# A one-layer encoder block on one core: latents turned in pieces, small first transfers, a tail in two tiles, weight halves side by side for the rotary key, and a second Strassen pair for B's output

## The chip, the core and the metric

The kernel runs on one core of a Trainium2 chip. The metric is the device time of one launch in microseconds (us). Three runs of the kernel before took 2494.61 to 2496.06 us, with a median of 2495.51. The core has five engines that run instruction streams of their own and in their own order: TensorE (PE, matmuls and transposes), VectorE (DVE), ScalarE (ACT), GpSimd (POOL) and SyncE (SP, here only a queue for transfers). An instruction that waits on its engine holds everything behind it on that engine.

## The reference

The block works on 256 tokens of width 2048 in float32. Cut to what matters:

```python
h = LN(alpha*h + 0.5*swiglu_ffn(h, ffn1_w_in, ffn1_w_out))      # d_ff 5504
proj = h @ w_in              # q, k, v of A | q_lat 512 | kv_lat 512 | k_pe 64 | gates
y_a = chunked_relbias_attention(q, k, v, rel_bias) @ w_o_a      # 16 heads of 64
c_q, c_kv = rms_norm(q_lat, q_a_norm), rms_norm(kv_lat, kv_a_norm)
k_pe = apply_rope(k_pe)                                         # one rotary key for all heads
y_b = mla_attention(c_q @ w_q_b, c_kv @ w_kv_b, k_pe) @ w_o_b   # 16 heads
h = LN(alpha*h + (sig(g_a)*y_a + sig(g_b)*y_b) @ w_out)
h = LN(alpha*h + cross_attention(h, LN(mem)))                   # 4 heads, 256 tokens of memory
out = LN(alpha*h + 0.5*swiglu_ffn(h, ffn2_w_in, ffn2_w_out))
```

## The kernel before

**Numbers in two halves.** Every operand of a matmul, weight or activation, is split into a high and a low half in the type fp32r, hi + lo. A product is three matmul passes: hi by hi, hi by lo, lo by hi. ACT casts the high half from the raw weights in casts of 1,024 columns (L242, in `halves`) and DVE subtracts to get the low half, 2,048 columns in one instruction (L245). For activations `split` does the same (L234, L235).

**Weights.** All weights stream once from memory, in 1 MB tiles of 128 rows by 2,048 columns (`raw`, three buffers) issued on SP's queue. `run` walks a list of items made with `add`; each item names the weights that it needs, and `run` fetches and splits weights ahead of it, with two units of hi and lo in flight. An item can have a priority: a positive one (SOON 400, NEAR 100) lets the scheduler put its instructions earlier among those of its engine, a negative one (LATE) later. The order on each engine is fixed when the kernel is built.

**Strassen pairs.** In a group of products (`pair_group`), the weights of two column blocks are multiplied with both token halves, eight products of blocks with three matmuls each, 24 matmuls of 512 columns for a step of two rows of weight blocks. At chosen steps (the tables `SUMS_...`) the group uses Strassen's seven products, 21 matmuls (`mm_sums`). Such a step needs sums of weight blocks (DVE, L189 and L191 in `form_sums`), a second split of these sums (ACT L242 and DVE L245 into a tile named X), and sums of the activations made once for all groups (`sum_forms`, called by `forms_step`). After the last such step `shared` joins the seven products (L627 to L632). `SUMS_YB` is the table of B's output projection, whose two groups are built by `out_b`; it has one pair, step 4.

**Wide products.** Where one weight tile turns features into features (`mm_wide`), the activation's hi and lo halves lie side by side, so that the high weights take 16 matmuls of 512 columns (L265) and the low weights 16 matmuls of 256 columns (L267), into the left half of the same bank. `total` adds the two halves of the bank (L273, L274).

**Start.** `start` runs 12 warm-up matmuls of ones (L475; the trace has two records for each), while the input `xT` (8 blocks of 256 KB) is asked for on ACT's queue (L483) and the first weights on SP's (L486, the first two tiles in halves). For each block it splits the input and then the weights, the high halves all on ACT, and multiplies.

**The mixer.** The order is: value and gates, then the latents (`w_lat`, whose product `lat_scale` scales by the root mean square, DVE L857 to L865), `gb_apply(0)`, the rotary key (`kpe`), A's first projections (`a_proj(0)`), `lat_turn`, A's heads and then B's heads. `lat_turn` turns the scaled latents with 16 transposes (L877), two into each bank half, and splits them from the bank: ACT for hi (L881) and DVE for lo (L882). B's projections read its result. `kpe` multiplies with `mm_wide`; its weight tile holds the 64 columns of the key twice, so that the 128 rows of the result are two copies. `swap` (L891) fetches a copy with neighbouring blocks of 32 rows exchanged, by four transfers on SP's queue; DVE multiplies by cosine and sine (L898, L899) and adds into `krope` (L902), which only B's scores (L924) read. `gb_apply(0)` applies the first norm's gain and bias to the residual `h`: for each quarter of 512 columns two broadcasts on POOL's queue (L440, L441) and four DVE operations (L444, L445).

**B's heads.** A loop over 16 heads issues for each the scores, the softmax on DVE and ACT (`softmax`), the transposes of the head before (L774), the projections of a head two ahead, and the head's output. After it come `out_a`, `out_b` and, beside B's output, the norm of the memory (`mem_norm`: statistics on DVE, L377 and L1167, spread over the partitions by PE at L1174).

**The end.** The last feed-forward's output is built by `out_pair` (columns 0 to 1,023) and `out_proj` (columns 1,024 to 2,047, groups of four weight blocks). `skewed` runs the last four weight groups for token half 0 first and then for token half 1, so that the first half's norm runs beside the second's matmuls. The last group of half 1 is 9 matmuls of 512 columns (L286); then DVE adds it to `h` (L701), takes the statistics (L377), joins them (L382), and `final_steps` normalizes and stores (L1320, L1321).

Of the kernel before, what the change touches and what calls it, by code (L numbers as in the profile page):

```python
# [91 lines left out]
class Kernel:  # L92
    def __init__(self, ctx, tc, t, out):
        self.tc, self.nc, self.t, self.out = tc, tc.nc, t, out

        def pool(name, bufs=1, **kw):
            return ctx.enter_context(tc.tile_pool(name=name, bufs=bufs, **kw))

        self.const = pool("const")
        self.wraw = pool("wraw", 3)  # L100
        self.whi = pool("whi", UNITS)
        self.wlo = pool("wlo", UNITS)
        self.blocks = pool("blocks")
# [7 lines left out]
        self.chain = None  # L111


# [165 lines left out]

    def mm_tok(self, ps, tt, w, x, kts, start, stop):  # L280

        n = len(kts)
        for wi in range(2):
            for j, kt in enumerate(kts):
                for xi in range(2 - wi):
                    self.last_mm = self.nc.tensor.matmul(  # L286
                        ps, x.at(xi, kt)[:, tt * P:(tt + 1) * P], w[wi][:, j * 512:(j + 1) * 512],
                        start=(start and j + wi + xi == 0), stop=(stop and j == n - 1 and wi == 1),
                    )
# [82 lines left out]

    def ln_begin(self):
        return self.small.tile([P, 4, 6], F32, tag="bn", name=self.name("bn"))

# [93 lines left out]
    def start(self):  # L469
# [6 lines left out]
        ps = self.group_tiles(0)  # L476
        xr = self.block("H0", (P, KT // 2, S)), self.block("H1", (P, KT // 2, S))
        for k in range(KT // 2):
            v = xr[k // 4][:, k % 4 * 2:k % 4 * 2 + 2, :]
# [12 lines left out]
            self.mm_pair(ps, w, 512, xT, (2 * k, 2 * k + 1), k == 0, k == KT // 2 - 1)  # L492
# [18 lines left out]
    def ffn(self, tag, xT, st, first=None, steps=None, late=None, before=None, tags=None):  # L511
# [6 lines left out]
        for half, nf in enumerate(F_SPLIT):  # L518
# [25 lines left out]
            if end and late:  # L544
                self.add(late)

            def out(hid=hid):
# [4 lines left out]
                if end:  # L552
                    self.out_proj(tag + "_w_out_r", nf, x, False, st, steps, tags, 2)
                else:
                    self.out_pair(bank ^ 1, src[1], 1, nf, x, homes, fh, half == 0, None)
# [139 lines left out]
    def finish(self, tt, n, ps, scale, st):  # L695
# [6 lines left out]
        if st is not None:  # L702
            if n == 0:
                st[tt] = self.ln_begin()
            self.ln_piece(st[tt], h[tt], n)

    def out_proj(self, wname, nk, x, scale, st, steps=None, tags=None, n0=0, other=False):

# [12 lines left out]
        def part(n, tts, i, ps, tags=None, held=0, keep=False, again=False):  # L721
            grp = groups[i]

            def fn(w=None):
                if keep:
                    kept[i] = w
                w = kept.pop(i) if again else w
                for tt in tts:
                    if i == 0:
                        ps[tt] = self.at_tile() if other and n == n0 else self.mm_tile()  # L730
                    self.mm_tok(ps[tt], tt, w, x(), grp, i == 0, i == len(groups) - 1)
                if i == len(groups) - 1:
# [51 lines left out]
    def mixer(self, xT, st, steps):  # L784
# [83 lines left out]

        def lat_turn():
            self.c = self.act(["X0", "X1"])  # L870
            for k in range(2):
                for b in range(2):
                    ps = self.at_tile()
                    for i in range(2):
                        j, p = 2 * b + i, ps[:, i * S:(i + 1) * S]
                        for tt in range(2):
                            nc.tensor.transpose(p[:, tt * P:(tt + 1) * P],  # L877
                                                self.lat[:, tt, k, j * P:(j + 1) * P], self.ident)
                        gain = self.vec(("q_a_norm", "kv_a_norm")[k], j)
                        hi, lo = (self.c.at(half, 4 * k + j) for half in (0, 1))  # L880
                        nc.scalar.mul(hi, p, gain)  # L881
                        nc.vector.scalar_tensor_tensor(lo, p, gain, hi.bitcast(F32), ALU.mult, ALU.subtract)  # L882

        self.pair_group(0, t["w_lat"][0], 512, KT, xT, SUMS_IN, fx, lps, lqs, None, SUM_HOME + ("H5",))
        self.add(lat_scale, prio=SOON)
        self.add(lambda: self.gb_apply(0, self.h), prio=LATE)

        def swap(dst, src):

            for b in range(4):  # L890
                nc.sync.dma_start(dst[32 * b:32 * b + 32], src[32 * (b ^ 1):32 * (b ^ 1) + 32])  # L891

        def kpe(w):
            ps = self.at_tile()
            self.mm_wide(ps, w, xT())
            a, b = self.total(ps), self.w1()
            swap(b, a)
            nc.vector.tensor_tensor(a, a, self.rope[:, 0, :], ALU.mult)  # L898
            nc.vector.tensor_tensor(b, b, self.rope[:, 1, :], ALU.mult)  # L899
            for j in range(2):  # L900
                rows = slice(64 * j, 64 * j + 64)
                nc.vector.tensor_tensor(self.krope[rows, j, :], a[rows], b[rows], ALU.add)  # L902
        self.add(kpe, t["w_kpe"][0])


        qk, sc, pt = {}, {}, {}
        oA = {}

        def a_proj(i):
            def one(k):  # L910
# [5 lines left out]
            for k in range(2):  # L916
                self.add(one(k), t["w_qk"][i, k])

        def scores(parts, spans_q):
# [82 lines left out]
        a_proj(0)  # L1002
        self.add(lat_turn)
        NA = A_HEADS // 2
# [69 lines left out]
        for h in range(B_HEADS + 1):  # L1074
# [8 lines left out]
            if h > 0:  # L1083
                b_out(h - 1, int(h % 2 == 0 and h + 2 < B_HEADS))


# [376 lines left out]
```

## Time and profile before

| What | Value |
|---|---|
| Runs, median and extent | 2495.51 us (2494.61 to 2496.06) |
| The profiled execution's own time | 2493.65 us |
| Its span | 2491.9 us |
| PE busy | 2471.8 us, 11,966 records |
| DVE busy | 2055.1 us, 82% |
| ACT busy | 1332.9 us, 53% |
| Memory read | 484.77 MB, 195 GB/s over the span |
| Clock granted to PE | full in all 40 slices |

In the timeline a row is the start in us, the length in us, engine, line, operation, output and inputs, the number of instructions in the row, and in brackets the idle time of the engine ahead of it with what released it. Successive matmuls overlap: the record of one with 512 columns is 0.39 us long, while the starts lie closer together. In the groups of instructions the numbers after the bar are the total busy us, the mean ns of one, and the idle time ahead. Windows list, for each stretch, the busy time of each engine with the number of records, then the clock, the share of the transfer engines and GB/s.

### The profile page before, as it was taken

To read this page: it belongs to the slowest core of one execution; us is meant where nothing else is said; L and a number is where in the kernel's file an instruction comes from. 1 tells how busy PE (TensorE), PEld (TensorE's weight loads), DVE (VectorE), ACT (ScalarE), POOL (GpSimd) and SP (SyncE) were. 2 spreads that over 40 slices of the span, in tenths; PEclk is the share of its full clock that TensorE was granted. 3 is DMA by queue.
4 is the path that set the end of the run, shared out by engine and by line. 5 is a ranking of instruction groups with operands and counts; after the bars stand their busy time and mean duration, and the time that the engine had idled before them with its cause. 6 is when DMAs were issued, how large, how long until landed. Compare 5 with 4: busy or idle time off the path is not lost.

```text
span 2491.9 us, 30464 instructions
## 1 busy us (share of the span) xinstructions
PE 2471.8 (99%) x11966; PEld 2082.8 (84%) x11966; DVE 2055.1 (82%) x2313; ACT 1332.9 (53%) x1798; POOL 28.8 (1%) x69
## 2 busy tenths in 40 slices
PE   9999999999999999999999999999999999999998
PEld 7888888889888888899888888898888888888886
DVE  6999889899778988676678798557888988898986
ACT  5555555555455555555445565545555555555552
POOL 0000000000000001000000000000000000000000
PEclk9999999999999999999999999999999999999999
DMA  7655555556645556543466557544555555655664
GB/s 255 240 191 208 188 201 209 203 186 204 236 160 203 210 203 226 199 153 119 168 221 219 186 175 247 189 167 148 205 204 186 203 186 203 210 198 201 206 211 141
DMA packets 72512, 490.03 MB, mean 197 GB/s; under 512 B 8368, under 2 KB 8752, under 8 KB 17200
## 3 DMA queue, kind: packets, MB, share of 16 engines
q1 hardware_dynamic: 66384, 467.11, 53.7%
q0 software_dynamic: 4256, 17.83, 2.2%
q10 hardware_dynamic: 1728, 3.15, 0.4%
q8 instruction: 93, 1.52, 0.2%
q14 instruction: 51, 0.42, 0.0%
HBM read 484.77 MB, written 2.10 MB: 195 GB/s over the span
## 4 chain that ended last, share of the span: by engine, by line
PE 95%; DVE 2%; DMA 1%; ACT 1%; issue 0%; SPq 0%; DVEq 0%; ACTq 0%; POOL 0%
PE mm L299 25%; PE at L299 25%; PE mm L353 10%; PE at L353 10%; PE mm L286 8%; PE mm L265 7%; PE mm L267 4%; PE mm L255 2%; PE at L924 1%; PE at L286 1%; DVE lo L245 1%; PE at L774 1%; DMA H<-xT 0%; PE at L1279 0%; PE at L404 0%; PE at L1255 0%
## 5 line engine op out<-in xcount | busy, mean ns | idle before, releaser
L242 ACT CAST hi<-raw 128x1024 fp32r<-128x1024 f32 (+1 forms) x848 | 801.8, 987 | 604.2 <-PE at L299 182.6
L245 DVE TENSOR_TENSOR lo<-raw,hi 128x2048 fp32r<-128x2048 f32 (+2 forms) x425 | 904.3, 2129 | 239.6 <-ACT hi L242 237.8
L299 PE MATMUL mm<-hi,T 128*128 128x512 f32 (+1 forms) x1280 | 298.4, 383 | 1.4 <-ACT hi L234 1.4
L242 ACT CAST X<-H 128x1024 fp32r<-128x1024 f32 (+1 forms) x162 | 164.9, 1034 | 216.7 <-DVE H L191 86.6
L299 PEld LDWEIGHTS mm<-hi,T 128*128 128x128 f32 x1280 | 238.0, 188 | 46.1 <-ACT hi L234 2.0
L299 PE MATMUL at<-hi,T 128*128 128x512 f32 x1072 | 257.0, 389 | 0.0
L245 DVE TENSOR_TENSOR X<-H,X 128x2048 fp32r<-128x2048 f32 (+1 forms) x81 | 182.3, 2251 | 67.7 <-ACT X L242 67.7
L299 PEld LDWEIGHTS at<-hi,T 128*128 128x128 f32 x1072 | 201.2, 188 | 41.9
L299 PE MATMUL mm<-lo,T 128*128 128x512 f32 (+1 forms) x640 | 153.8, 382 | 0.0
L299 PE MATMUL at<-hi,H 128*128 128x512 f32 x608 | 144.7, 390 | 0.9 <-DVE w L632 0.9
L299 PEld LDWEIGHTS mm<-lo,T 128*128 128x128 f32 x640 | 119.1, 188 | 21.8
L299 PEld LDWEIGHTS at<-hi,H 128*128 128x128 f32 x608 | 113.9, 188 | 24.7 <-DVE w L632 1.3
L299 PE MATMUL at<-lo,T 128*128 128x512 f32 x536 | 132.6, 389 | 0.0
L265 PE MATMUL mm<-T,hi 128*128 128x512 f32 x512 | 124.4, 394 | 0.0
L299 PEld LDWEIGHTS at<-lo,T 128*128 128x128 f32 x536 | 100.6, 188 | 20.9
L299 PE MATMUL mm<-hi,H 128*128 128x512 f32 x480 | 116.1, 392 | 0.0
L191 DVE TENSOR_TENSOR H<-H,raw 128x512 f32<-128x512 f32 (+1 forms) x162 | 109.5, 676 | 1.7
L265 PEld LDWEIGHTS mm<-T,hi 128*128 128x128 f32 x512 | 94.2, 189 | 19.3 <-issue 0.9
L299 PEld LDWEIGHTS mm<-hi,H 128*128 128x128 f32 x480 | 89.3, 188 | 18.2 <-DVE w L274 0.2
L189 DVE TENSOR_TENSOR H<-raw 128x1024 f32<-128x1024 f32 (+1 forms) x81 | 97.1, 1199 | 3.0 <-DMA raw<-ffn_w_in 1.7
L353 PE MATMUL mm<-X,X 128*128 128x512 f32 x348 | 95.9, 392 | 0.0
L242 ACT CAST X<-raw 128x1024 fp32r<-128x1024 f32 (+1 forms) x54 | 55.4, 1035 | 51.5 <-DVE raw L191 31.9
(321 smaller groups left out, 3913.9 us busy)
## 6 DMA issues: line engine op xcount, KB each, us to landing
raw<-ffn_w_in SPq DMA_DIRECT2D x150, 1024.0 KB, 4.8
raw<-ffn_w_out SPq DMA_DIRECT2D x66, 1024.0 KB, 4.8
raw<-w_gate SPq DMA_DIRECT2D x32, 1024.0 KB, 4.8
raw<-ffn_w_out_r SPq DMA_DIRECT2D x16, 1024.0 KB, 4.9
raw<-w_qk SPq DMA_DIRECT2D x16, 1024.0 KB, 4.8
raw<-w_o_b SPq DMA_DIRECT2D x16, 1024.0 KB, 4.8
raw<-w_out SPq DMA_DIRECT2D x16, 1024.0 KB, 4.8
raw<-w_xk SPq DMA_DIRECT2D x16, 1024.0 KB, 4.8
```

The source lines that it names most:

```text
L189: self.nc.vector.tensor_tensor(two[0], two[1], raw[:, :m].unsqueeze(1).to_broadcast([P, 2, m]), ALU.add)
L191: self.nc.vector.tensor_tensor(t[:, a * m:a * m + m], t[:, b * m:b * m + m], raw[:, a * m:a * m + m], ALU.add)
L242: self.nc.scalar.copy(hi[:, c:d], src[:, c:d])
L245: self.nc.vector.tensor_tensor(lo[:, :n], src, hi[:, :n].bitcast(F32), ALU.subtract)
L255: self.nc.tensor.matmul(ps, w[wi][:, cols[j]:cols[j] + P], x.at(xi, kt), start=(j + wi + xi == 0), stop=(j == n - 1 and wi == 1),)
L265: self.nc.tensor.matmul(ps, hi[kt], x.both(kt), start=(kt == 0), stop=False)
L267: self.last_mm = self.nc.tensor.matmul(ps[:, :S], lo[kt], x.at(0, kt), start=False, stop=(kt == n - 1))
L286: self.last_mm = self.nc.tensor.matmul(ps, x.at(xi, kt)[:, tt * P:(tt + 1) * P], w[wi][:, j * 512:(j + 1) * 512], start=(start and j + wi ...
L299: self.last_mm = self.nc.tensor.matmul(ps[tt, g][:, :n], x.at(xi, kt)[:, tt * P:(tt + 1) * P], w[wi][:, c:c + n], start=first and j + wi + ...
L353: self.last_mm = self.nc.tensor.matmul(bank[:, :m], a[xi], v[wi][:, c * m:(c + 1) * m], start=own and first and wi + xi == 0, stop=own and ...
L774: self.nc.tensor.transpose(ps[:, i * P:(i + 1) * P], s[:, c:c + P], self.ident)
L924: nc.tensor.matmul(ps[:, c0:c0 + nk], q[:, tt * P:(tt + 1) * P], k[:, :nk], start=(j == 0), stop=(j == len(parts) - 1))
```

## The change

1. **Start.** The input's blocks 0 to 2 are all asked for at the front on ACT's queue, block 0 in two halves of 128 KB; blocks 3 to 7 go on SP's queue between the weights, two tiles ahead. The first weight tile comes in four transfers of 256 KB, the second in two of 512 KB. Block 0's high half is cast by DVE, half by half.
2. **Rotary key.** The weight tile holds the key's 64 columns twice. An ACT copy puts the low half's right 64 columns into the right half of the high tile, so that 16 matmuls of 512 columns make both products: rows 0 to 63 from the high weights, rows 64 to 127 from the low ones. The two have to be added across rows: two transfers (64 rows each) on POOL's queue exchange the halves, and DVE adds. Then `swap` runs as before, but on POOL's queue.
3. **Latents.** `lat_turn` becomes four pieces of four transposes, each after one projection of A's head pairs 1 and 2.
4. **First norm's gain and bias.** `gb_apply(0)` moves from ahead of `kpe` into B's loop, a quarter at heads 2, 5, 8 and 11.
5. **B's output.** `SUMS_YB` has a second pair, step 6, so each group has three matmuls fewer; the sums of the activations of heads 12 and 13 are made too.
6. **Tail.** In the last feed-forward the second-last weight group of token half 1 ends its bank, which is added to `h` at once; the last group runs as two tiles of 256 columns (18 matmuls in place of 9), each with an add and statistics of its own, so that token half 1 has five pieces of statistics.

```diff
-SUMS_YB = {4: ("T0", 0)}
+SUMS_YB = {4: ("T0", 0), 6: ("T0", 1)}
...
-    def ln_begin(self):
-        return self.small.tile([P, 4, 6], F32, tag="bn", name=self.name("bn"))
+    def ln_begin(self, n=4):
+        return self.small.tile([P, 5, 6], F32, tag="bn", name=self.name("bn"))[:, :n, :]
...
-    def gb_apply(self, i, h):
+    def gb_apply(self, i, h, qs=range(4)):
...
-        for q in range(4):
+        for q in qs:
...
+        def x_load(q, k, step=2):
+            for i in range(0, 2, step):
+                q.dma_start(v[k][:, i:i + step, :], t["xT"][:, 2 * k + i:2 * k + i + step, :])
+        for k in range(3):
+            x_load(nc.scalar, k, 2 if k else 1)
...
-            nc.scalar.dma_start(v, t["xT"][:, 2 * k:2 * k + 2, :])
-            for c in range(0, 2048, 1024 if k < 2 else 2048):
-                d = c + (1024 if k < 2 else 2048)
-                nc.sync.dma_start(raw[:, c:d], src[:, c:d])
-            self.split(v, xT.blk(0, 2 * k, 2), xT.blk(1, 2 * k, 2))
+            n = (512, 1024, 2048)[min(k, 2)]
+            for c in range(0, 2048, n):
+                nc.sync.dma_start(raw[:, c:c + n], src[:, c:c + n])
+            if 2 < k + 2 < KT // 2:
+                x_load(nc.sync, k + 2)
+            for i in range(0, 2, 1 if k == 0 else 2):
+                m = 1 if k == 0 else 2
+                hi, lo = (xT.blk(a, 2 * k + i, m) for a in (0, 1))
+                if k == 0:
+                    nc.vector.tensor_copy(hi, v[k][:, i:i + m, :])
+                    nc.vector.tensor_tensor(lo, v[k][:, i:i + m, :], hi.bitcast(F32), ALU.subtract)
+                else:
+                    self.split(v[k], hi, lo)
...
+                if cut and again and i == len(groups) - 1:
+                    for a in range(2):
+                        p = self.mm_tile()
+                        self.mm_tok(p[:, :S], 1, w, x(), grp, True, True, a * S, S)
+                        hs = h[1][:, n * 512 + a * S:n * 512 + a * S + S]
+                        with self.prio(SOON):
+                            nc.vector.tensor_tensor(hs, hs, p[:, :S], ALU.add)
+                            nc.vector.bn_stats(st[1][:, 3 + a, :], hs)
+                    return
...
+                    short = cut and again and i == len(groups) - 2
+                    self.mm_tok(ps[tt], tt, w, x(), grp, i == 0, short or i == len(groups) - 1)
+                    if short:
+                        hs = h[tt][:, n * 512:(n + 1) * 512]
+                        nc.vector.tensor_tensor(hs, hs, ps[tt], ALU.add)
...
+        def lat_turn(k, b):
+            def fn():
+                if k + b == 0:
+                    self.c = self.act(["X0", "X1"])
+                ps = self.at_tile()
+                for i in range(2):
...
-        self.add(lambda: self.gb_apply(0, self.h), prio=LATE)
...
         def kpe(w):
+            both = w[0].rearrange("p (k m) -> p k m", k=KT)
+            with self.prio(SOON):
+                nc.scalar.copy(both[:, :, 64:], w[1].rearrange("p (k m) -> p k m", k=KT)[:, :, 64:].bitcast(F32))
             ps = self.at_tile()
-            self.mm_wide(ps, w, xT())
+            for kt in range(KT):
+                nc.tensor.matmul(ps, both[:, kt, :], xT().both(kt), start=(kt == 0), stop=(kt == KT - 1))
             a, b = self.total(ps), self.w1()
-            swap(b, a)
+            for j in range(2):
+                nc.gpsimd.dma_start(b[64 * j:64 * j + 64], a[64 * (1 - j):64 * (1 - j) + 64])
+            nc.vector.tensor_tensor(a, a, b, ALU.add)
+            c = self.w1()
+            swap(c, a, nc.gpsimd)
...
-        self.add(lat_turn)
...
-                a_proj(i + 1)
+                a_proj(i + 1, [lat_turn(i, b) for b in range(2)] if i < 2 else ())
...
+            if h in (2, 5, 8, 11):
+                self.add(lambda q=h // 3: self.gb_apply(0, self.h, (q,)), held=int(h % 2 == 0), prio=LATE)
...
-        self.add(self.forms_step(fb, SUMS_YB, 4, lambda: oB["t"]))
+        for c in SUMS_YB:
+            self.add(self.forms_step(fb, SUMS_YB, c, lambda: oB["t"]))
```

More of the change, by code (lines that the diff above doesn't have):

```diff
@@ L545, in ffn @@
                 self.add(late)
+                self.add(lambda: setattr(self, "cut", True))
             def out(hid=hid):
@@ L703, in finish, with out_proj @@
             if n == 0:
-                st[tt] = self.ln_begin()
+                st[tt] = self.ln_begin(5 if self.cut and tt else 4)
             self.ln_piece(st[tt], h[tt], n)
-    def out_proj(self, wname, nk, x, scale, st, steps=None, tags=None, n0=0, other=False):
+    def out_proj(self, wname, nk, x, scale, st, steps=None, tags=None, n0=0, other=False, cut=False):
         nc, t, h = self.nc, self.t, self.h
@@ L867, in lat_scale @@
                         nc.scalar.mul(l, l, r)
[L869 to L880, printed above, removed]
+        def lat_turn(k, b):
[4 more added lines that the diff above has]
+                for i in range(2):
+                    j, p = 2 * b + i, ps[:, i * S:(i + 1) * S]
+                    for tt in range(2):
+                        nc.tensor.transpose(p[:, tt * P:(tt + 1) * P],
+                                            self.lat[:, tt, k, j * P:(j + 1) * P], self.ident)
+                    gain = self.vec(("q_a_norm", "kv_a_norm")[k], j)
+                    hi, lo = (self.c.at(half, 4 * k + j) for half in (0, 1))
+                    with self.prio(NEAR):
@@ L898, in kpe @@
+            nc.vector.tensor_tensor(a, a, b, ALU.add)
+            c = self.w1()
+            swap(c, a, nc.gpsimd)
             nc.vector.tensor_tensor(a, a, self.rope[:, 0, :], ALU.mult)
-            nc.vector.tensor_tensor(b, b, self.rope[:, 1, :], ALU.mult)
+            nc.vector.tensor_tensor(c, c, self.rope[:, 1, :], ALU.mult)
             for j in range(2):
                 rows = slice(64 * j, 64 * j + 64)
-                nc.vector.tensor_tensor(self.krope[rows, j, :], a[rows], b[rows], ALU.add)
+                nc.vector.tensor_tensor(self.krope[rows, j, :], a[rows], c[rows], ALU.add)
@@ L907, in mixer, with a_proj @@
         oA = {}
-        def a_proj(i):
+        def a_proj(i, side=()):
             def one(k):
@@ L917, in a_proj @@
                 self.add(one(k), t["w_qk"][i, k])
+                for f in side[k:k + 1]:
+                    self.add(f)
         def scores(parts, spans_q):
```

15 lines of the change are left out of this document (8 added, 7 removed).

## The prediction

> **What bounds the kernel now.** I read the page first, then PE's waits, then the timeline around each wait. The page gives busy time and share of the span for each engine, and the chain of work that ended last:
>
> ```profile
> PE 2471.8 (99%) x11966; PEld 2082.8 (84%) x11966; DVE 2055.1 (82%) x2313; ACT 1332.9 (53%) x1798; POOL 28.8 (1%) x69
> PE 95%; DVE 2%; DMA 1%; ACT 1%; issue 0%; SPq 0%; DVEq 0%; ACTq 0%; POOL 0%
> ```
>
> PE is busy for 2471.8 of 2491.9 us. So time can come out of three places only: fewer or narrower matmuls, PE's few waits, and the ends before the first real matmul and after the last. The waits of PE (total, number, longest, in us):
>
> ```profile
> PE at L877 <- DVE X L882: 3.6, 1, 3.6
> PE mm L299 <- ACT hi L234: 1.4, 2, 0.8
> ```
>
> The first is in the turning of the latents (`lat_turn`), the second is two waits in the first 15 us. Both lie where the change works. Nothing else on the list exceeds 1.1 us, so the whole change can be worth some ten microseconds, and I go through it piece by piece.
>
> **The change part by part.** *Rotary key.* Timeline rows (start, length, engine, line):
>
> ```profile
> 944.46 2.29 DVE L245 TENSOR_TENSOR lo<-raw,hi 128x2048 fp32r<-128x2048 f32 x1
> ...
> 947.57 2.01 ACT L242 CAST hi<-raw 128x1024 fp32r<-128x1024 f32 x2 [3.72 <-PE mm L299]
> ...
> 949.18 3.79 PE L265 MATMUL at<-T,hi 128*128 128x512 f32 x16
> ...
> 952.81 2.08 PE L267 MATMUL at<-T,lo 128*128 128x256 f32 x16
> ...
> 954.72 3.82 PE L265 MATMUL mm<-T,hi 128*128 128x512 f32 x16
> ```
>
> The 16 matmuls of 512 columns take 952.81 - 949.18 = 3.63 us (0.227 each), the 16 of 256 columns 954.72 - 952.81 = 1.91 us (0.12 each). The change drops the second sixteen: -1.9. It adds an ACT copy of 1,024 elements, about 1.05 us by the casts of that size (2.01 for two), which cannot begin before DVE's low part ends, 944.46 + 2.29 = 946.75. ACT is idle there (3.72 us up to 947.57), so the copy ends near 947.8, ahead of 949.18 by 1.4 us. Without that cover it costs its own 1.05. Value -1.9, bounds -1.9 and -0.9.
>
> *Latents in pieces.* The same stretch later, with the transfers of that window (KB each, us to landing):
>
> ```profile
> 951.10 2.28 DVE L245 TENSOR_TENSOR lo<-raw,hi 128x2048 fp32r<-128x2048 f32 x1
> ...
> 952.25 0.55 POOL L441 DMA_DIRECT2D w<-gb  x1
> ...
> 955.97 0.69 DVE L444 TENSOR_TENSOR h<-h,w 128x512 f32<-128x512 f32 x1 [1.84 <-DMA w<-gb]
> ...
> 957.78 2.49 SPq L891 DMA_DIRECT2D w<-w  x4
> ...
> 965.23 0.43 DVE L898 TENSOR_TENSOR w<-w,rope 128x256 f32<-128x256 f32 x1 [1.71 <-DMA w<-w]
> ...
> 965.86 1.04 PE L877 MATMUL at<-ident,H 128*128 128x128 f32 x8
> ...
> 969.93 2.28 DVE L245 TENSOR_TENSOR lo<-raw,hi 128x2048 fp32r<-128x2048 f32 x1
> ...
> 972.46 2.91 DVE L882 SCALAR_TENSOR_TENSOR X<-at,vecs,X 128x256 fp32r<-128x256 f32 x7
> 972.99 0.44 PE L877 MATMUL at<-ident,H 128*128 128x128 f32 x2 [3.58 <-DVE X L882]
> ...
> 975.65 0.48 DVE L882 SCALAR_TENSOR_TENSOR X<-at,vecs,X 128x256 fp32r<-128x256 f32 x1 [0.29 <-ACT X L881]
> w<-gb POOLq DMA_DIRECT2D x8, 256.0 KB, 6.1
> w<-w SPq DMA_DIRECT2D x4, 32.0 KB, 5.7
> ```
>
> Eight transposes go through, two for each of the four banks; a bank's second two wait until DVE has read its first (L882), and DVE stands in a 2.28 us low part that ends at 972.2, so PE idles 3.58 us. The seven reads that follow occupy DVE to 975.4, which is why the transposes after 972.99 come in twos with single matmuls between. In the changed kernel a piece is one bank: two transposes, a DVE read of 0.48, two more, with the matmuls of one projection between pieces. By its order DVE's read still stands behind a 2.28 us low part in two of the four pieces: I put 0.5 on each, so -3.6 becomes -3.6 + 1.0, and the disturbance after 972.99 gives back some 0.4: -3.0. The bound on the good side is all of it with the disturbance, -4.4. The bound on the other side comes from the key's transfers: the product halves are now added through two POOL transfers (64 rows each), and the swap follows with four more, where one hop stood on SP. One hop took from 957.78 to 965.23, and DVE waited 1.71 us at its end. The two DVE instructions that wait for the hops stand in DVE's order ahead of the low parts of the next two projections' weights and of the latents' reads. At 5.7 to 6.1 us a hop, both in series, DVE can stand long enough that a stall like the old one (up to 3.4) is back: -0.5.
>
> *Gain and bias of the first norm* (`gb_apply(0)`). Its 16 adds and multiplies leave this stretch and go to B's heads 2, 5, 8 and 11, four at each, between the steps of the softmax chains:
>
> ```profile
> L444 DVE TENSOR_TENSOR h<-h,w 128x512 f32<-128x512 f32 x24 | 15.7, 684 | 1.8 <-DMA w<-gb 1.8
> ...
> 1150.00:1170.00 20.00, 19.95 (x134) 18.11 (x132) 13.62 (x33) 9.97 (x25) 0.00 (x0) 1.00 0.32 106
> 1170.00:1190.00 20.00, 19.95 (x143) 18.53 (x140) 13.94 (x34) 11.42 (x30) 0.21 (x1) 1.00 0.37 119
> ```
>
> The second row's columns are the stretch, then busy time of PE, PEld, DVE, ACT, POOL. A quarter is 4 x 0.684 = 2.74 us of DVE. DVE is busy 13.6 to 13.9 of 20 us here, so about 1.6 us of every head's 5.3 are free, 4.9 for three heads: the work fits. But an add that is begun just before a chain step delays that step by up to 0.68, and PE already shows 0.05 us of idle per 20. I take 0.2 for each quarter: +0.8, between -0.4 (waits of PE here vanish with the new order) and +3 (one full add on PE's path per quarter).
>
> *B's output, second Strassen pair.* A group does three products fewer: 24 becomes 21, and there are two groups, so 6 x 0.227 = -1.4. DVE gains, for each group, the sums of the weights and their low part:
>
> ```profile
> L189 DVE TENSOR_TENSOR H<-raw 128x1024 f32<-128x1024 f32 x75 | 91.4, 1219 | 3.0 <-DMA raw<-ffn_w_in 1.7 <-DMA raw<-w_gate 1.1
> ...
> 1280.00:1300.00 20.00, 20.00 (x98) 16.79 (x97) 19.72 (x19) 10.90 (x14) 0.55 (x1) 1.00 0.66 244
> 1300.00:1320.00 20.00, 20.00 (x90) 16.58 (x89) 19.55 (x41) 8.04 (x10) 1.07 (x2) 1.00 0.81 284
> ...
> 1319.96 0.28 DVE L1167 TENSOR_SCALAR w<-ident,y 128x128 f32<-128x128 f32 x1
> ...
> 1350.37 1.05 PE L1174 MATMUL at<-w,w 128*128 128x128 f32 x8
> ```
>
> That is 1.22 + 2 x 0.68 + 2.29 = 4.9 us. For the first group DVE has room. The second falls into 1280 to 1320, where DVE has 0.28 + 0.45 = 0.7 us free in 40. What gives way there is the statistics of the memory, which end with L1167 at 1319.96 and are used by PE at 1350.37, 30 us later. So it is hidden at -1.4; if instead the low parts of PE's weights slip, it costs up to 4.9 - 0.7 = 4.2 against 1.4 won: +2.8.
>
> *The start.*
>
> ```profile
> 1.06 4.78 PE L475 MATMUL at<-w 128*128 128x128 f32 x24 [1.06 <-DVE w L451]
> ...
> 5.48 0.62 ACT L234 CAST T<-H 128x512 fp32r<-128x512 f32 x1 [2.79 <-DMA H<-xT]
> ...
> 6.67 3.99 PE L299 MATMUL mm<-hi,T 128*128 128x512 f32 x16 [0.83 <-ACT hi L234]
> ...
> 13.23 0.62 ACT L234 CAST T<-H 128x512 fp32r<-128x512 f32 x1 [2.99 <-DMA H<-xT]
> ...
> 13.75 1.04 ACT L234 CAST hi<-raw 128x1024 fp32r<-128x1024 f32 x1
> ...
> 14.85 1.43 PE L299 MATMUL mm<-hi,T 128*128 128x512 f32 x5 [0.56 <-ACT hi L234]
> ```
>
> The input's block lands at 5.48, is cast (0.62), then ACT casts the first weights, and PE begins at 6.67, having waited 0.83 after the warm-up. With 128 KB and 256 KB pieces and the input's cast on DVE, data and casts can be there before the warm-up ends at 1.06 + 4.78 = 5.84, and the warm-up is unchanged, so at most 0.83 to 0.95 is won. The wait of 0.56 at 14.85 exists because ACT stood 2.99 us for the third input block before it cast the weights at 13.75; that block is now asked for at the very start. Value -1.5 (0.9 + 0.6), bounds -1.7 and -0.6 (the second wait alone).
>
> *The tail.*
>
> ```profile
> L274 DVE TENSOR_TENSOR w<-w,mm 128x256 f32<-128x256 f32 x48 | 19.8, 413 | 0.3
> ...
> 2475.49 2.73 DVE L1321 SCALAR_TENSOR_TENSOR h<-h,y,T 128x512 f32<-128x512 f32 x4
> 2479.48 0.69 DVE L701 TENSOR_TENSOR h<-h,mm 128x512 f32<-128x512 f32 x1 [1.25 <-PE mm L286]
> 2480.20 0.69 DVE L377 BATCH_NORM_STATS2 bn<-h 128x6 f32<-128x512 f32 x1
> ```
>
> After the last matmul DVE runs an add and the statistics of 512 columns, 2 x 0.69. Of 256 columns the add is 0.41, and I take the same for the statistics, so 0.55 is won. Eighteen matmuls of 256 columns take 18 x 0.12 = 2.16 where nine took 9 x 0.227 = 2.04: +0.1. The additional early add (0.69) fits DVE's 1.25 us of idle time ahead of 2479.48. Net -0.45, bounds -0.6 and -0.2.
>
> **Sum:** -1.9 - 3.0 + 0.8 - 1.4 - 1.5 - 0.45 = -7.4 us. The profiled execution took 2493.65 (span 2491.9 and 1.75 around it), so it would be 2486.2. The median of the runs is 2495.51, 1.9 above it (0.07%); against that the sum gives 2488.1, which I predict.
>
> **The rivals.** (a) *The key's two hops hold DVE.* For it: DVE runs in order, and in the trace it already waited 1.71 us for one hop. Against it: nothing on PE needs the key before B. Then a stall of some 3.4 stays in place of the 3.6: 2488.1 + 3.4 = 2491.5. That it lasts longer on POOL's queue isn't in the rows: POOL issued a transfer at 952.25 in 0.55 us while DVE ran the low part from 951.10 to 953.38. The Trainium skill ("SBUF — State Buffer", section "SBUF: two separate sides") says that a DMA from the POOL queue appears blocked while DVE runs an operation in a 2-port mode, since its descriptors cannot be written; here the trace does not bear it out, and by the rule each hop would last a low part (about 2.3) longer.
>
> (b) *Small first transfers gain nothing.* Then the first matmul stays at 6.67 and the start gives 0.6; with the tail at its lower bound the time is 2488.1 + 0.9 + 0.25 = 2489.3. For it: 6.67 is only 0.83 after the warm-up, and more transfers run side by side, each slower. The Trainium skill ("DMA: Bandwidth & Descriptors", section "Bandwidth") speaks for this rival: transfers should be batched to 1 MiB or more, and 64 KB is mostly overhead. Against it: the first cast needs only a quarter of the weights and half the input block.
>
> (c) *Strassen's second pair does not hide*, because low parts of PE's weights slip between 1280 and 1320: +2.8 in place of -1.4, so 2488.1 + 4.2 = 2492.3. For it: 0.7 us free in 40. Against it: 30 us of slack in the memory's statistics.
>
> (d) *Slower: the quarters in B hold DVE.* DVE's order is fixed, so if a quarter's broadcast has not landed DVE stands, and the head's softmax behind it, and PE behind that. At 955.97 such a wait was 1.84. With its four operations (2.74) on PE's path a quarter costs 4.6, four cost 18.3, against 8.2 won elsewhere: 2495.5 + 10.1 = 2505.6. It decides from 8.2 / 4 = 2.05 a quarter on. Against it: POOL has nothing else to do in B, so the broadcasts are issued early, and DVE has 1.6 us free in a head.
>
> **How the numbers follow.** Forecast 0.61, (a) 0.13, (b) 0.09, (c) 0.12, (d) 0.05. A change under 0.2% (5.0 us) cannot be told from none: the limit is 2490.5. Above it lie (a) and (c), 0.25, and below it the rest of the four. From the forecast's own spread I move a little over the limit and from (a) and (c), where they are half as dear, a little back: faster 0.72, same 0.23, slower 0.05. The range takes the forecast's good bounds together in part (2485) and reaches past (c) to 2492.7; outside are (d) and the ends of the bounds.
>
> **What would show it.** Right: PE's wait at L877's successor under 1 us each; the first L299 matmul before 6.0 and no wait at the third block; 16 fewer matmuls after the key's L265 row; DVE's last add and statistics near 0.41 each; no new wait of PE on DVE in B. Wrong: a wait of PE over 2 us on the low parts near 960 to 975 (a), the first matmul still near 6.67 (b), waits of PE on L245 between 1280 and 1320 (c), waits on the softmax at heads 2, 5, 8 or 11 (d).

## The result, and the profile after

| | Median of six runs | Profiled execution (its span) |
|---|---|---|
| before | 2495.33 us (2494.61 to 2496.06) | 2493.65 us (2491.9) |
| changed | 2485.77 us (2485.13 to 2489.82) | 2485.13 us (2483.4) |

The ratio of the runs is 0.9963 with a 95% interval of 0.9952 to 0.9974: 9.6 us faster, more than the 5.0 us under which a change could not be told from none, and inside the predicted range of 2485.0 to 2492.7. The predicted 2488.1 was 2.3 us too high: about 1.1 because the two profiled executions differ by 8.5 us where the parts had added up to 7.4, and most of the rest because the profiled execution of before lay 1.9 us under its median and that of the changed kernel only 0.6 under.

The page of the changed kernel, busy time per engine and the chain that ended last:

```profile
PE 2467.4 (99%) x11953; PEld 2079.9 (84%) x11953; DVE 2066.2 (83%) x2334; ACT 1337.6 (54%) x1803; POOL 31.8 (1%) x75
PE 93%; DVE 3%; DMA 2%; ACT 1%; issue 1%; DVEq 0%; ACTq 0%
```

PE is still the bound, with 4.4 us less work. PE's waits in the changed kernel (total, number, longest):

```profile
PE mm L354 <- DVE H L236: 1.7, 1, 1.7
...
PE at L802 <- DVE w L797: 0.6, 1, 0.6
...
PE mm L287 <- DVE lo L246: 0.3, 1, 0.3
```

The wait on the latents (3.6) is gone, and so is the one of the start (1.4). A wait of 1.7 us has come up in the last feed-forward, at a place that the change does not touch. The 0.6 at L802 stands in B's heads, where the kernel before shows no wait.

**How the parts are read.** Run times can't tell parts of a microsecond apart here: the kernel before alone had medians of 2494.5, 2494.7 and 2495.7 us in three sets of runs, and the intervals below are about 3 us to each side. So I use two quantities of the trace. *Position* is the start of a landmark on PE, compared between kernels: the first transposes of the hidden values (L690 before, L705 after, near 62 us), the transposes of A's softmax (L774, L802), those of B's output (L1118, L1158). *PE's loss* in a stretch is the sum over PE's matmuls of the time from one start to the next, less the normal pitch for the width of the first (0.227 us for 512 columns, 0.173 for 384, 0.120 for 256, 0.109 for 128). Between 930 and 1000 us, which holds the key and the latents, PE's loss was 5.65 us before and 1.22 after.

By positions, before less after (times of the kernel before, but for the wait): 1.17 us at 62 us (the start), 1.45 at 949 (some tenths more from waits at the first norm), 7.83 at the second group of A's transposes, called A's second head pair below (1009.99 against 1002.16), 8.16 after B's first output group and 8.87 after the second, 8.77 at 1846, 7.03 at 1889 (the wait of 1.7), 8.49 at 2388, 7.82 at the start of the last weight group, 8.13 when the last statistics are joined, 8.5 at the end.

### The profile page after: what moved, and what is told of

It reads as the page before. It is cut to its first block, busy times and chain, and to the rows that moved or that the text cites. A ratio compares the mean times of both kernels' runs of the same rounds, so it can differ in the third digit from the quotient of the medians.

```text
span 2483.4 us, 30482 instructions
## 1 busy us (share of the span) xinstructions
PE 2467.4 (99%) x11953; PEld 2079.9 (84%) x11953; DVE 2066.2 (83%) x2334; ACT 1337.6 (54%) x1803; POOL 31.8 (1%) x75
## 3 DMA queue, kind: packets, MB, share of 16 engines
q10 hardware_dynamic: 1152, 1.84, 0.2%
## 4 chain that ended last, share of the span: by engine, by line
PE 93%; DVE 3%; DMA 2%; ACT 1%; issue 1%; DVEq 0%; ACTq 0%
PE mm L300 26%; PE at L300 24%; PE mm L354 10%; PE at L354 10%; PE mm L266 7%; PE mm L287 5%; PE mm L268 4%; PE mm L256 2%; DVE lo L246 1%; PE at L963 1%; DMA raw<-ffn_w_out_r 1%; PE at L802 1%; DMA raw<-w_xo_r 1%; PE at L1320 0%; PE at L405 0%
```

## The experiments

**Gain and bias back ahead of the key** (`x_gb`).

```diff
         self.add(lat_scale, prio=SOON)
+        self.add(lambda: self.gb_apply(0, self.h), prio=LATE)
...
-            if h in (2, 5, 8, 11):
-                self.add(lambda q=h // 3: self.gb_apply(0, self.h, (q,)), held=int(h % 2 == 0), prio=LATE)
```

> The changed kernel with the first norm's gain and bias back ahead of the rotary key, in one piece; the latents stay in four pieces. Theory (the pieces removed PE's stall): PE's total of start-to-start time over its normal pitch between 930 and 1000 us stays near the changed kernel's 1.2 us, and the 0.35 us that B's heads lost comes back, so 2485.4 us against 2485.8. Rival (the 16 DVE operations of 0.69 us, 11 us in all, made the stall by standing ahead of the latents' reads): 2 to 3.6 us of the stall return, 2488 to 2489.4.

Measured: 2492.25 us (2491.36 to 2494.26), ratio to before 0.999 (0.998 to 0.9999); PE's loss between 930 and 1000 is 8.84 us. More than the whole stall is back, although the latents are in pieces. The timeline:

```profile
952.99 1.05 POOL L932 DMA_DIRECT2D w<-w  x2 [0.52 <-DVE ly L362]
...
955.27 0.69 DVE L445 TENSOR_TENSOR h<-h,w 128x512 f32<-128x512 f32 x1 [2.49 <-DMA w<-gb]
...
962.39 0.43 DVE L933 TENSOR_TENSOR w<-w,w 128x256 f32<-128x256 f32 x1 [3.34 <-DMA w<-w]
...
967.75 1.34 ACT L895 ACTIVATE H<-H,ly 128x512 f32<-128x512 f32 x2 [4.09 <-DVE ly L371]
...
976.03 0.69 PE L905 MATMUL at<-ident,H 128*128 128x128 f32 x2 [5.17 <-DVE X L911]
```

DVE stands 2.49 us for a broadcast of the gain and 3.34 us for the key's first hop, which takes from 952.99 to 962.39. Behind these stands the rest of the root mean square (`ly`), so the latents are scaled at 967.75, and PE waits 5.17 us. The same rows of the changed kernel:

```profile
952.68 1.08 POOL L931 DMA_DIRECT2D w<-w  x2 [2.67 <-DVE ly L362]
...
958.62 0.43 DVE L932 TENSOR_TENSOR w<-w,w 128x256 f32<-128x256 f32 x1 [2.40 <-DMA w<-w]
...
959.16 1.34 ACT L895 ACTIVATE H<-H,ly 128x512 f32<-128x512 f32 x2 [1.98 <-DVE ly L371]
...
971.09 0.44 PE L905 MATMUL at<-ident,H 128*128 128x128 f32 x2
```

There the hop takes 5.9 us, DVE still stands 2.40 us for it, the latents are scaled 8.6 us earlier, and PE does not wait. The theory that the pieces had removed the stall falls; the rival has the cause, and the stall is longer than it forecast. Not the whole 11 us lay in the way: ahead of the read that ends PE's wait stood nine of the sixteen operations, 6.1 us, and as much again of DVE's waits for transfers (2.49, 3.34 and 0.30).

**Latents in one step** (`x_lat`), and **both back** (`x_gblat`, the two edits together).

```diff
         a_proj(0)
+        self.add(lat_turn)
...
-                a_proj(i + 1, [lat_turn(i, b) for b in range(2)] if i < 2 else ())
+                a_proj(i + 1)
```

The body of `lat_turn` goes back too, and with it the priority NEAR that the changed kernel gives to the reads of the banks; the two are not parted.

> The changed kernel with the latents turned in one step after A's first projections, as before; gain and bias stay in B's heads. Theory (pieces): the stall of 3.6 us and its disturbance come back, 4.4 us, so 2490.2. Rival (gain and bias): DVE has 11 us less to do in the stretch, the reads of the banks come at once and under 1 us returns, 2486.8 or less.

> The changed kernel with both back: gain and bias ahead of the key and the latents in one step; the new key, with two hops on POOL's queue, stays. Theory and rival alike: the stall is back, 4.4 us, less the 0.35 of B's heads, 2489.8. If the two hops hold DVE longer than the one hop of before did, the stall is longer than 3.6, up to 7, and the time up to 2493.

Measured: `x_lat` 2487.88 us (2485.12 to 2488.63), PE's loss 4.23; `x_gblat` 2491.75 us (2490.75 to 2494.77), PE's loss 9.60. Each profile is that of the slowest run. In `x_lat`:

```profile
958.80 0.43 DVE L930 TENSOR_TENSOR w<-w,w 128x256 f32<-128x256 f32 x1 [2.79 <-DMA w<-w]
...
967.94 0.44 PE L905 MATMUL at<-ident,H 128*128 128x128 f32 x2 [2.13 <-DVE X L910]
```

And PE's longest wait in `x_gblat` (total, number, longest):

```profile
PE at L905 <- ACT H L895: 6.7, 1, 6.7
```

So by these profiles pieces are worth 4.23 - 1.22 = 3.0 us beside the new key when gain and bias are away, and 9.60 - 8.84 = 0.8 when they are there. Neither is firm in the run times. Two of the five runs of `x_lat` took 2485.1 and 2485.6 us, no longer than the changed kernel, and the median of `x_gblat` lies 0.5 below that of `x_gb`. `x_lat` lies between theory and rival. In `x_gblat` the last clause came true: PE waits 6.7 us, longer than the 3.6 of before. DVE stands 4.02 us there for the new key's first hop (the add at 964.84), where before it stood 1.71 for the one hop.

**The kernel before with gain and bias moved, and nothing else** (`x_before_gb`).

```diff
-        self.add(lambda: self.gb_apply(0, self.h), prio=LATE)
...
+            if h in (2, 5, 8, 11):
+                self.add(lambda q=h // 3: self.gb_apply(0, self.h, (q,)), held=int(h % 2 == 0), prio=LATE)
```

> The kernel before with one part of the change, gain and bias in four quarters in B's heads; the key with its one hop, the latents in one step. Theory (the 11 us of DVE work and the broadcasts made most of the stall): of 5.65 us over PE's normal pitch between 930 and 1000 us some 3.0 are left or fewer, and with 0.4 lost in B the time is 2492.4. Rival (the stall was the one-step turning, and gain and bias matter only beside the new key's two hops): 5 us or more are left there, 2494.5 or more.

Measured: 2489.59 us (2487.98 to 2492.99), ratio 0.9977 (0.9967 to 0.9987): this one edit gives 6.1 of the 9.9 us by which the changed kernel led in the same set of runs (2485.76 against 2495.70). PE's loss is 0.41 us, less than in any other run:

```profile
957.55 2.49 SPq L890 DMA_DIRECT2D w<-w  x4
...
963.38 0.42 DVE L897 TENSOR_TENSOR w<-w,rope 128x256 f32<-128x256 f32 x1
...
965.56 1.03 PE L877 MATMUL at<-ident,H 128*128 128x128 f32 x8
...
968.46 3.36 DVE L882 SCALAR_TENSOR_TENSOR X<-at,vecs,X 128x256 fp32r<-128x256 f32 x8
...
968.99 0.44 PE L877 MATMUL at<-ident,H 128*128 128x128 f32 x2
```

The latents are turned in one step, the second transposes come 3.4 us after the first, and PE has other work until then. DVE waits for no hop (no bracket at L897). DVE's reads of the banks begin at 968.46, in the kernel before at 972.46. The stall of before was made by gain and bias, not by the one-step turning: the theory holds and more than holds. By position the edit is worth 5.2 us at both of B's output groups (1327.07 against 1332.28 at the second). How much of it is DVE's operations and how much the broadcasts' slowing of other transfers, no run parts.

**The key's transfers on SP's queue**, in the changed kernel (`x_sp`) and with gain and bias back (`x_gbsp`).

```diff
-                nc.gpsimd.dma_start(b[64 * j:64 * j + 64], a[64 * (1 - j):64 * (1 - j) + 64])
+                nc.sync.dma_start(b[64 * j:64 * j + 64], a[64 * (1 - j):64 * (1 - j) + 64])
...
-            swap(c, a, nc.gpsimd)
+            swap(c, a)
```

> The changed kernel with the key's six transfers on SP's queue in place of POOL's. Theory (nothing on PE waits for the key before B's heads, and DVE's wait of 2.4 us for the first hop is covered): no change, 2485.5 to 2486.1, with DVE's waits for the two hops as long as now or some tenths different. Rival (SP's queue holds the weights' loads behind the transfers, which wait there for DVE's sums): PE waits 1 us or more on weights between 960 and 985, 2487 or more.

> Gain and bias ahead of the key, latents in pieces, and the key's six transfers on SP's queue. With POOL's queue the first hop took 9.4 us from issue to DVE's add, without the broadcasts 5.9. Theory (the hop stands in POOL's queue behind the broadcasts): on SP's queue it takes 6 us or less, PE's stall falls from 5.2 to 2.5 us or less, 2489. Rival (the broadcasts slow every transfer, whatever its queue): 8 us or more and the stall stays, 2491.5 or more.

Measured: `x_sp` 2485.28 us (2483.45 to 2485.49), PE's loss 1.16: no change of the time, as the theory had it, though DVE's wait for the first hop is gone with the other order. `x_gbsp` 2492.26 us (2489.44 to 2493.61), PE's loss 8.06, its wait 3.8 us in place of 5.2: the rival, though the wait is shorter. The transfers between 949 and 966 us, KB each and us to landing, in the changed kernel, in `x_gb` and in `x_gbsp`:

```profile
raw<-w_qk SPq DMA_DIRECT2D x3, 1024.0 KB, 4.8
w<-w POOLq DMA_DIRECT2D x2, 64.0 KB, 5.4
w<-w POOLq DMA_DIRECT2D x4, 32.0 KB, 1.7
```

```profile
raw<-w_qk SPq DMA_DIRECT2D x3, 1024.0 KB, 7.4
w<-gb POOLq DMA_DIRECT2D x6, 256.0 KB, 7.1
w<-w POOLq DMA_DIRECT2D x2, 64.0 KB, 8.6
```

```profile
raw<-w_qk SPq DMA_DIRECT2D x3, 1024.0 KB, 8.5
w<-gb POOLq DMA_DIRECT2D x7, 256.0 KB, 6.8
w<-w SPq DMA_DIRECT2D x2, 64.0 KB, 11.0
```

Beside the broadcasts a 64 KB hop takes 8.6 us on POOL's queue and 11.0 on SP's, where it stands behind a weight tile that is slowed as well (4.8 to 8.5). So the broadcasts slow the transfers on both queues, and taking the hop off POOL's queue does not help. Whether standing behind the broadcasts in POOL's queue adds to the 8.6, these runs do not show.

**What a long wait cost beside itself.** PE's loss is more than its wait, and the granted clock shows why. Windows of the kernel before, its wait and a stretch behind it, and the second stretch in `x_before_gb`:

```profile
969.40:972.99 3.59, 0.01 (x1) 0.00 (x0) 3.59 (x6) 0.00 (x0) 0.00 (x0) 1.00 0.72 240
974.32:977.73 3.41, 3.41 (x16) 3.08 (x15) 2.73 (x6) 2.69 (x5) 0.00 (x0) 0.50 0.58 245
```

```profile
974.32:977.73 3.41, 3.41 (x22) 2.98 (x20) 1.68 (x2) 0.83 (x1) 0.00 (x0) 1.00 0.34 60
```

Behind the wait the kernel before ran for 3.41 us at a granted clock of 0.50, too short to show among the 40 slices of the page. PE counts as busy there, but matmuls of 512 columns start 0.427 us apart in place of 0.227. That is about 1.6 us of the loss of 5.65 (an estimate: 0.2 of each 0.427 over 3.41 us). The same happened in `x_gb` and `x_lat` (3.41 us at 0.50) and in `x_gblat` and `x_gbsp` (6.83 us), the other profiles in which PE waited 2.1 us or more. It did not in the nine whose longest wait past the start was 1.7 us or less.

**The key as before** (`x_kpe`), **one Strassen pair** (`x_yb`), **the start as before** (`x_start`), **the tail as before** (`x_tail`): the parts of the change taken back one at a time. Their edits are the change's own hunks turned round; of the two short ones:

```diff
-SUMS_YB = {4: ("T0", 0), 6: ("T0", 1)}
+SUMS_YB = {4: ("T0", 0)}
...
-self.add(lambda: setattr(self, "cut", True))
+pass
...
-self.out_proj(tag + "_w_out_r", nf, x, False, st, steps, tags, 2, cut=tags is None)
+self.out_proj(tag + "_w_out_r", nf, x, False, st, steps, tags, 2, cut=False)
```

> The changed kernel with the rotary key as before: 32 matmuls, one hop on SP's queue. Theory (the sixteen matmuls of 256 columns are the whole price, and the copy and the two hops are covered): 1.9 us slower than the changed kernel, 2487.7. Rival (the two hops cost something that the trace of PE does not name, by holding DVE 2.4 us at the first): under 1.5 us slower, 2487.2 or less.

> The changed kernel with one Strassen pair in B's output. Theory (six matmuls fewer, all else hidden): 1.36 us slower, 2487.1, and PE's offsets to the changed kernel differ by 0.68 after each of the two groups. Rival (DVE's 4.9 us a group delay later work, the memory's norm or the weights): under 0.7 us slower or faster, 2486.4 or less.

> The changed kernel with the start as before. Theory (0.5 us at the first matmul in that execution, 0.7 at the weights' second half): 1.2 us slower, 2487.0, the wait of 0.6 to 0.7 near 14.8 us is back. Rival (the first matmul is set by the warm-up, whose matmuls ran at 0.21 us each until 4.9 us in one profile and beyond 6.2 in the other, and so by chance): 0.7 us slower, 2486.5.

> The changed kernel with the tail as before: one add and statistics of 512 columns after nine matmuls. Theory: 0.3 to 0.5 us slower, 2486.1 to 2486.3, and the statistics are joined 1.8 to 1.9 us after the last matmul's start, where the halves take 1.35. Rival (the end is set by the output's transfers): no difference.

| Run | Median, us | Its ratio to before | Position against the changed kernel |
|---|---|---|---|
| `x_kpe` | 2486.49 | 0.9965 (0.9952 to 0.9978) | +1.9 at A's second head pair |
| `x_yb` | 2485.47 | 0.9961 (0.9946 to 0.9976) | +0.67 from A's last head to the first group, +0.68 more after the second |
| `x_start` | 2486.00 | 0.9964 (0.9950 to 0.9977) | +1.2 at 62 us |
| `x_tail` | 2485.06 | 0.9959 (0.9945 to 0.9973) | statistics joined 3.69 us after the last group's start, in place of 3.38 |

The medians lie within 0.8 us of the changed kernel's and settle nothing: none shows the slower time that its theory gave, and two are lower. The positions agree with the first three theories; the tail's halves are worth 0.31 (from the last matmul's start the statistics take 1.88 us with one tile and 1.35 with two, as forecast, but the last matmul starts later). What the medians hide is the last feed-forward. In the changed kernel a weight tile lands late there, DVE and then PE wait for it:

```profile
1829.27 1.23 DVE L190 TENSOR_TENSOR H<-raw 128x1024 f32<-128x1024 f32 x1 [2.42 <-DMA raw<-ffn_w_in]
...
1843.93 1.66 PE L354 MATMUL mm<-X,X 128*128 128x512 f32 x6 [1.69 <-DVE H L236]
raw<-ffn_w_in SPq DMA_DIRECT2D x2, 1024.0 KB, 5.7
```

and in `x_kpe`, where the same two tiles take 4.7 us, DVE waits 1.06 us and PE has no such wait:

```profile
1829.00 1.22 DVE L190 TENSOR_TENSOR H<-raw 128x1024 f32<-128x1024 f32 x1 [1.06 <-DMA raw<-ffn_w_in]
...
raw<-ffn_w_in SPq DMA_DIRECT2D x2, 1024.0 KB, 4.7
```

That wait cost PE between nothing and 1.9 us in the fourteen profiles taken of these kernels, and all of `x_kpe`'s 1.9 us is given back there (its position at 1882 is even 0.15 ahead of the changed kernel's). Near 2372, at a wait of 1.0, it falls behind again, and it ends 1.1 us behind. So the positions show that PE gets through these parts earlier; that the launch ends earlier by as much is not shown. Why these tiles land sooner or later is open.

For the start, `x_tail`, which has the new one, shows why an earlier first matmul is not a gain by itself:

```profile
1.06 4.55 PE L476 MATMUL at<-w 128*128 128x128 f32 x24 [1.06 <-DVE w L452]
...
5.49 2.18 PE L300 MATMUL mm<-hi,T 128*128 128x512 f32 x8
...
7.67 1.27 ACT L235 CAST hi<-raw 128x512 fp32r<-128x512 f32 x2 [1.71 <-DMA raw<-ffn_w_in]
...
8.34 1.84 PE L300 MATMUL mm<-hi,T 128*128 128x512 f32 x6 [0.67 <-ACT hi L235]
```

and the changed kernel's own profile:

```profile
1.06 5.49 PE L476 MATMUL at<-w 128*128 128x128 f32 x24 [1.06 <-DVE w L452]
...
6.21 4.14 PE L300 MATMUL mm<-hi,T 128*128 128x512 f32 x16
...
11.99 3.79 PE L300 MATMUL mm<-hi,T 128*128 128x512 f32 x16
```

The first began 0.7 us earlier, then waited at 8.34 for the third quarter of the weights, and was 0.3 us *later* at 62 us (61.27 against 60.96). `x_out` began at 5.48 and was at 60.83, so an early beginning does not always lose either.

**The changed kernel again** (`x_after`, unedited) and **gain and bias in A's output projection** (`x_out`).

```diff
-        for g in range(2):
-            out_a(g)
+        main = self.collect(lambda: [out_a(g) for g in range(2)])
+        quarter = lambda q: (lambda: self.gb_apply(0, self.h, (q,)))
+        self.weave(main, {i: [quarter(q)] for q, i in enumerate((2, 4, 7, 9))}, prio=LATE)
```

> The changed kernel again, unedited, on the chip of these runs, where the kernel before takes 2494.5 to 2494.7 us in place of 2495.3: 2485.0 us. PE's position at 60 us, past the start, and its waits in the last feed-forward show how much of a few tenths is chance: I expect the same start of the matmuls after the latents to 0.3 us and waits between 1800 and 2480 us that differ by up to 1.5 us.

> The changed kernel with gain and bias taken out of B's heads once more and put into A's output projection, a quarter at each of four steps, where DVE is busy 45 to 75% and no softmax stands behind it. Theory (the quarters cost PE 0.4 us in B's heads): 0.4 us faster than the changed kernel, 2484.6, and the two waits of PE on L797 are 0.4 us each as in the kernel before. Rival (the quarters cost nothing, the order differs for another reason): no difference.

Measured: `x_after` 2485.76 us (2485.65 to 2486.87), `x_out` 2485.53 us (2485.13 to 2487.53): no difference that can be told. `x_after` took 0.8 us more than expected and stood 0.33 us from the first profile of the changed kernel at 1002 us, about the 0.3 expected. PE's losses at its two stops behind L797 in `x_out` are back at 0.4 us each, against 0.3 and 0.7 in `x_after`, and from A's second head pair to the end of B's first output group PE takes 276.91 us against 277.19, so 0.3 us were won there. They do not show at the end: this execution stood 0.3 us behind at 1002 us already, after a longer wait at the first norm (0.83 against 0.56), and lost 0.4 more in the wait near 1844 (1.9 against 1.4). No version tried is clearly faster than the changed kernel.

## Why the prediction was right, step by step

- *Rotary key, -1.9.* Right: the position moves by 1.9 when it is taken back. The copy stood where it was put, ACT L925 at 945.32 for 1.06 us, ahead of the matmuls at 947.73. But the hops have a price, which the prediction put into the bound of the next step and into rival (a): beside the one-step turning they cost PE 4.23 - 0.41 = 3.8 us in the profiled run (`x_lat` against `x_before_gb`), more than the matmuls save. With the pieces, the key and the pieces together gave 1.9 - (1.22 - 0.41) = 1.1 us over gain and bias moved alone.
- *Latents in pieces, -3.0.* This is the step that failed in its reason. The stretch gave 5.65 - 1.22 = 4.4, the good bound, but not through the pieces. Moving gain and bias alone took 5.65 to 0.41. The pieces are needed only because of the new key's hops; beside the old key they cost 1.18 - 0.41 = 0.8 (`x_kpe` against `x_before_gb`). I had read the low part ahead of L882 as the cause. DVE came late to it and to the reads because seven of the sixteen gain-and-bias operations (4.8 us), a wait of 1.84 for a broadcast and one of 1.71 for the hop stood ahead; without them the reads begin 4.0 us earlier. The "disturbance" was mis-sized and misread too: it was not 0.4 to 0.8 but 5.65 - 3.74 = 1.9 (3.74 is the wait with the drain of the matmul ahead of it), mostly the half clock behind the wait. That is a fourth place for time, which the list of three left out. That the sum held here is luck: the time came out of the stretch, but by the next part of the change, and with gain and bias left in place the pieces gave 0.8 (9.60 - 8.84, beside the new key).
- *Gain and bias, +0.8.* From the landmark at 1071 to B's first output group the changed kernel takes 208.53 us and `x_gb` 208.13: +0.4, mis-sized by half (between 0.1 and 0.6 in the pairs of profiles with and without it). The sign that no new wait of PE on DVE would come up in B failed by the 0.6 at L802. Booked only as a cost, it was the largest gain of the change.
- *Strassen, -1.4.* Right: 0.67 and 0.68. The memory's statistics gave way, and PE waited for nothing between 1240 and 1325.
- *Start, -1.5.* Mis-sized: 61.0 on average at 62 us in the eleven profiles with the new start (60.8 to 61.4) against 62.1 in the three with the old, so -1.1. The first matmul came at 5.5 to 6.2; the sign said before 6.0, which seven of the eleven profiles miss, the changed kernel's own with 6.21 among them, since the warm-up, taken as unchanged, lasted longer there. Where it came early, part was given back in `x_tail` at the third quarter of the weights. The wait of 0.56 is gone. Rival (b) had its reason half right: in `x_tail` the landing of weights decided, not the first matmul.
- *Tail, -0.45.* 0.31. The early add ended at 2471.0, and the first half's add and statistics ran straight behind it:

```profile
2470.32 0.68 DVE L759 TENSOR_TENSOR h<-h,mm 128x512 f32<-128x512 f32 x1
2471.10 0.42 DVE L749 TENSOR_TENSOR h<-h,mm 128x256 f32<-128x256 f32 x1
...
2471.90 0.40 DVE L749 TENSOR_TENSOR h<-h,mm 128x256 f32<-128x256 f32 x1
2472.34 0.43 DVE L750 BATCH_NORM_STATS2 bn<-h 128x6 f32<-128x256 f32 x1
```

  DVE was still busy with the first half when the second half's matmuls ended, so the second add began late; the step had left this out.
- *Sum.* The parts as measured: -1.2 - 1.9 - 4.4 + 0.4 - 1.35 - 0.3 = -8.75, against -7.4 forecast and 8.5 between the two profiles; in between lie the wait of 1.7 at 1844, less one of 0.9 at 2378 that of these two only the profile of before has, 0.3 us of small waits before 930, and 0.4 after the last statistics (8.13 to 8.5).
- *Rivals.* (a), the hops hold DVE, is a real mechanism: DVE waited 2.40 us, but with gain and bias away and the latents in pieces nothing stood behind it that PE needed in time. With gain and bias there PE waited 3.8 to 6.7 us. Its price of 3.4 was added to a forecast that had kept 1.0 of a stall already; by the bound of -0.5 in place of -3.0 it is 2.5, so 2490.6. (c) and (d) did not occur. The hops were no slower on POOL's queue than on SP's (5.4 against 5.8 us in `x_sp`, 8.6 against 11.0 beside broadcasts). The Trainium skill's rule on POOL's queue ("SBUF — State Buffer", section "SBUF: two separate sides") speaks of DVE operations in a 2-port mode; no row here shows in which mode the low parts ran, so neither the prediction's remark nor these runs test it.

## What to carry to other kernels

Before crediting the instruction next to a stall, remove the other work on the same in-order engine in that stretch, in the kernel before and alone: here one line moved gave 6.1 of 9.9 us in one set of runs, and the key and the pieces beside it gave 1.1 together. Broadcasts of a small tensor were large transfers here (256 KB each), and beside them weight tiles landed after 7.4 to 8.5 us in place of 4.8, so put them where nothing waits on a short hop. Look at the granted clock behind a long wait of PE: here it was at half for 3.4 to 6.8 us after such waits, and the page's busy share did not show it. Where run medians scatter by a microsecond, compare the positions of landmarks on the bounding engine instead.

## What the runs showed that was not expected

- *The warm-up runs at two speeds.* Its records start 0.213 us apart at first and 0.112 later; in seven of the fourteen profiles the switch lies between 4.4 and 5.3 us, in the other seven not before the last warm-up at 6.13. The page's clock row shows full speed throughout, but the record of the granted clock begins only with the switch, at 4.45 us in `x_tail` and, as the latest, at 7.08 in `x_yb`, where the first two real matmuls still ran slowly (0.57 and 0.38 us). The Trainium skill ("TensorE: Matmul & The Clock Gate", Part 1) says that the gate opens after a busy window of about 3.4 us that runs freely, so that the moment varies from run to run; with matmuls from 1.06 us the range of 4.45 to 7.08 agrees with that. How early the first real matmul can come is thus partly chance.
- *Transfers slowed one another.* On POOL's queue 32 KB landed after 1.7 us with the weight tiles alone in flight and after 3.0 in `x_gb`, beside broadcasts; a 1 MB weight tile took 4.8 us with only the hops beside it and 8.5 in `x_gbsp`.
